# State-space mixer: the swap split from the state step and tied behind a GELU, four weight loads tied behind the returning quarters, the plan redrawn

## The chip, the cores and the metric

The kernel runs on one core of one Trainium2 chip. The metric is the device time of one execution in microseconds (us); several runs are taken and their median is compared. Beside the runs there is one profiled execution, from which every row below comes. TensorE is PE in the rows (PEld is its weight load), VectorE is DVE, ScalarE is ACT, GpSimd is POOL, and SyncE, which issues all the DMAs here, is SP.

## The reference

A two-layer decoder trunk on 512 tokens of width 1024, in float32: layer 0 mixes by convolution and attention, layer 1 by a state-space layer, and after each comes a gated MLP with a short convolution. The part around the change is the state-space mixer:

```python
u = (rms_norm(x) @ w_in).reshape(b, s, 32, 16)          # 512 wide, 32 groups of 16 channels
bu = einsum(u, B)                                       # each group feeds 64 complex states
x  = associative_scan(combine, (lam, bu))               # x[t] = lam * x[t-1] + bu[t], complex
y  = Re(C x) + D * u
y  = gelu(y)
z  = y @ w_glu + b_glu                                  # 512 -> 2048
return z[..., :1024] * sigmoid(z[..., 1024:])
```

## The kernel before

**Operands.** Every large weight comes in chunks of 128x1024 float32 (512 KB). `load_w` issues the DMA on SP into one of two `raw` buffers, `split_w` casts the chunk to a high part `whi` on ACT (three buffers) and takes the rest `wlo` on POOL in four pieces. Three matmuls (high by high, high by low, low by high) then stand for one float32 product. `chunk` hands out the chunks in a fixed order and keeps two loads ahead (`LOOK = 2`): after the last chunks of the first MLP come the four chunks of `w1` (the mixer's input projection), the eight of `wg` (the GLU), and then the second MLP. For a few chunks the cast is tied behind the newest ACT copy (`newest[0]`) at the point where the chunk is asked for.

**Who sets the order.** A scheduler orders the instructions of each engine by its own timeline. In the mixer all matmuls (`mm`) are held in program order, and `behind(a, b)` forces `a` after `b` on one engine without a wait between engines. Each engine, and SP's queue of DMAs, then works strictly in its order: an instruction that waits holds all behind it.

**The mixer in quarters.** The 512 channels are four quarters of eight groups. Time is cut into 64 chunks of 8 steps. For quarter q:

- dense: 24 matmuls of the input projection give `pss[q]` (quarters 0 and 1 run first, together, 48 matmuls; then quarter 2, then quarter 3);
- `s5_move`: ACT copies it to `u`, a DMA writes it to DRAM (`du`), and a second DMA (`moved[q]`) reads it back transposed into `rs[q]` (`r` in the rows); DVE scales it by the row norms (`s5_scale`);
- `E` (`s5_state`): 64 small matmuls on PE give `e1` and `e2`; DVE makes `za`, `zb`, their sum and the scan `z`; `swap` exchanges the two halves of the partitions with two ACT copies into `zs`; DVE makes `za`, `zs` (`turned`) and the state `xs`;
- `T` (`s5_direct`): 16 matmuls of `r` with table `tabT` into `y`; `O` (`s5_out`): 16 matmuls of `xs` with `tabO` added to `y`;
- `Y` (`s5_turn`): GELU on ACT (`ya`), 32 small matmuls that turn it (`yt`), then ACT and DVE split it into the operand of the GLU;
- `t` (`load_tables`): two DMAs of 512 KB each fetch the tables of quarter q, tied behind `moved[q]`.

**The plan.** A string gives the order on PE. `D24` means up to 24 more matmuls of the stream "dense projection of quarters 2 and 3, then GLU parts"; `A1`, `A2`, `A3` allow the GLU parts of quarter 0, 1, 2. The GLU parts are 12 matmuls of quarter 0, 12 of quarter 1, 6 and 6 more of these, and 18 of quarter 2. A `D` that meets a part which isn't allowed yet ends there. So in the plan before the dense runs are 24, 12, 6, 6, then 12, 12, 6, 6 (the second `D12` after `T3` stops at 6) and none after `O3`.

```python
PLAN = "D24 t1 E0 D12 t2 E1 T0 D6 O0 T1 D6 Y0 E2 t3 A1 D12 O1 Y1 T2 E3 A2 D12 O2 D6 Y2 T3 D12 O3 D12 Y3 A3"
```

After the plan the remaining GLU matmuls run, chunk by chunk, with the sigmoid and the product on ACT and DVE.

Of the kernel before, what the change touches and what calls it, by code (L numbers as in the profile page):

```python
# [38 lines left out]
E0 = 2  # L39
# [4 lines left out]

PLAN = "D24 t1 E0 D12 t2 E1 T0 D6 O0 T1 D6 Y0 E2 t3 A1 D12 O1 Y1 T2 E3 A2 D12 O2 D6 Y2 T3 D12 O3 D12 Y3 A3"
RA, RB2, GN = (26, 22, 6)
LAST = ("b", "sc", "pt", "b", "sc", "pt", "sc", "pt")
WT, WP, UT, UP = (8, 3, (2, 2, 1), (2, 1))  # L50
# [3 lines left out]
S0, S1 = (42, 16)  # L54
# [18 lines left out]
def trunk(ctx, tc, A, out):  # L73
    nc = tc.nc
    v, s, g, pe = nc.vector, nc.scalar, nc.gpsimd, nc.tensor
# [12 lines left out]
    def bank(name, tag=None):  # L88
        if tag is None:
            tag = CYCLE[turn[0] % len(CYCLE)]  # L90
            turn[0] += 1
        return pp.tile([128, T], F32, tag=tag, bufs=TAGS[tag], name=name)
# [4 lines left out]
    def tmp(name="t", shape=(128, T), dt=F32):  # L97
        return tp.tile(list(shape), dt, tag="t", bufs=6, name=name)
# [4 lines left out]
    def behind(ins, first):  # L103
        tc.add_manual_dep(ins.ins, first.ins.name, mybir.DependencyInfo(
            mybir.DependencyClass.NoSync, mybir.DependencyReason.DATA), reason="order on one engine")
# [3 lines left out]
    def mm(*a, **kw):  # L109
        r = pe.matmul(*a, **kw)  # L110
        return held(r) if fixed[0] else r

    def load_w(src, n):
        raw = wp.tile([128, 1024], F32, tag="raw", bufs=WB, name="raw")
        nc.sync.dma_start(out=raw[:, :n * 128], in_=src)
        return raw

    def split_w(raw, n, eng=None, keep=None, after=None):
        if keep:
            hi, lo = (keep.tile([128, n, 128], F32R, tag=t, bufs=KD - 1, name=t) for t in ("khi", "klo"))  # L120
        else:
            hi = wp.tile([128, 8, 128], F32R, tag="whi", bufs=3, name="whi")
            lo = wp.tile([128, 8, 128], F32R, tag="wlo", bufs=3, name="wlo")
        r = raw[:, :n * 128].rearrange("p (k m) -> p k m", m=128)
        cast = s.copy(hi[:, :n], r)  # L125
        if after:
            behind(cast, after)
        for a in range(0, n, 2):
            (eng or g).tensor_tensor(lo[:, a:a + 2], r[:, a:a + 2], hi[:, a:a + 2].bitcast(F32), ALU.subtract)  # L129
        return hi, lo  # L130

    order = [(A["w0"][m], 8) for m in range(12)]
    order += [(A["wukv"], 8), (A["wuq"][0], 8), (A["wuq"][1], 8)]
    order += [(A[n][c], 8) for n, c in (("wo_a", 0), ("wo_a", 1), ("wo_a", 2), ("wo_c", 0), ("wo_a", 3),
# [10 lines left out]
    first_w1 = len(order)  # L145
# [8 lines left out]
    def chunk(src, n=8):  # L154
        i = taken[0]
        assert order[i][1] == n and order[i][0].tensor is src.tensor and order[i][0].offset == src.offset
        if i == first_w1 + 2:
            queue[i + 1] = split_w(queue[i + 1], 8, after=newest[0])
        while len(queue) <= min(i + LOOK, len(order) - 1):
            j = len(queue)  # L160
            raw = load_w(*order[j])
            if j == first_w1 + 3:
                queue.append(raw)
                continue
            queue.append(split_w(raw, order[j][1], keep=kept[0] if stay <= j < stay + KD - 1 else None,
                                 after=newest[0] if first_w1 + 2 <= j <= first_w1 + 6 else None))
        taken[0] += 1
        res, queue[i] = queue[i], None
        return res
# [24 lines left out]
    for step in START:  # L194
        if step[0] == "x":
            k = int(step[1])
# [82 lines left out]
    def xhi():  # L279
        return xp.tile([128, T], F32R, tag="xh", bufs=8, name="xh")  # L280

    def xlo():
        return xp.tile([128, T], F32R, tag="xl", bufs=8, name="xl")
# [75 lines left out]
    for step in START:  # L359
        if step[0] == "x":  # L360
            k = int(step[1])
# [15 lines left out]
    with tc.tile_pool(name="l0", bufs=1) as lp:  # L377
        def slot(name, dt=F32):
            return lp.tile([128, T], dt, tag="m", bufs=16, name=name)
# [3 lines left out]
        def w_in(m):  # L383
            fill(WT, WP)
            if m in early:
                return early[m]
            return proj(bank("win", ("sc", "b")[m % 2]), chunk(A["w0"][m]), n0.hl)
# [107 lines left out]
        for i in range(2):  # L495
            ps = w_in(M_Q + i)
            t = slot(f"cq{i}")
# [20 lines left out]
        for t in (cq[0], cq[1], ckv):  # L518
            q = tmp("sq")
# [126 lines left out]
        for i in range(4):  # L646
            v.scalar_tensor_tensor(y[i], mb, -1.0 / CW, y[i], ALU.mult, ALU.add)
            q = tmp("sq")
# [303 lines left out]
    def ztmp(name):  # L952
        return fp.tile([128, T], F32, tag="z", bufs=ZB, name=name)
# [50 lines left out]
                elif extra:  # L1004
                    extra.pop(0)()

    tTs, tOs, moved = [], [], {}

    def load_tables(q):
        gq = slice(8 * q, 8 * q + 8)  # L1010
        for lst, n in ((tTs, "T"), (tOs, "O1")):
            t = fp.tile([128, 8, 128], F32, tag="ghl", bufs=GB, name="tab" + n)
            d = nc.sync.dma_start(out=t, in_=park[n][:, gq])
            if q:
                behind(d, moved[max(q, 1)])
            lst.append(t)
# [6 lines left out]
    tE, tC, tS, tD = tab["E"], tab["C"], tab["S"], tab["D"]  # L1023

    def as_g(t):
        return t.rearrange("p (g c) -> p g c", c=NC)

    lo, hi = slice(0, 64), slice(64, 128)
    pss, rs, xs, yb, ys = {}, {}, {}, {}, []
    late, done_r = [], []  # L1030

    def s5_move(q):
# [11 lines left out]
    def s5_scale(q):  # L1044
        v.tensor_tensor(rs[q], rs[q], rowr.unsqueeze(1).to_broadcast([128, 8, NC]), ALU.mult)

    def swap(dst, src):
        s.copy(dst[lo], src[hi])
        newest[0] = s.copy(dst[hi], src[lo])

    def s5_state(q):
        gq = slice(8 * q, 8 * q + 8)
        cf, sf = (t[:, gq].rearrange("p g c -> p (g c)") for t in (tC, tS))
        e1, e2 = bank("e1", "b"), bank("e2", "b")
        for e, other in ((e1, (lo, hi)), (e2, (hi, lo))):
            for i in range(8):
                for a, to in zip((lo, hi), other):
                    mm(e[to, i * NC:(i + 1) * NC], tE[:, 8 * q + i, a], rs[q][:, i], start=True, stop=True)
        za, zb, z, zs = ztmp("za"), ztmp("zb"), ztmp("z"), ztmp("zs")
        v.tensor_tensor(za, e1, cf, ALU.mult)  # L1060
        v.tensor_tensor(zb, e2, sf, ALU.mult)
        v.tensor_tensor(za, za, zb, ALU.add)
        v.tensor_tensor_scan(z, tD[:, gq].rearrange("p g c -> p (g c)"), za, 0.0, ALU.mult, ALU.add)
        swap(zs, z)
        x_ = ztmp("xs")
        xs[q] = as_g(x_)
        g.memset(xs[q][:, :, 0:1], 0.0)
        v.tensor_tensor(za, z, cf, ALU.mult)
        turned(zs, sf)
        v.tensor_tensor(xs[q][:, :, 1:], as_g(za)[:, :, :NC - 1], as_g(zs)[:, :, :NC - 1], ALU.subtract)  # L1070

    def turned(t, sf):
        v.tensor_tensor(t, t, sf, ALU.mult)
# [7 lines left out]
    def s5_direct(q):  # L1081
        yb[q] = bank("y", "pt")
        table(yb[q], tTs[q], rs[q], True, False)

    def s5_out(q):
        table(yb[q], tOs[q], xs[q], False, True)

    def s5_turn(q):
        ya = tmp("ya")
        gelu = s.activation(ya.rearrange("p (j g c) -> p g j c", j=CL, c=GC),  # L1090
                     yb[q].rearrange("p (g j c) -> p g j c", j=CL, c=GC), AF.Gelu_apprx_tanh)
        if q == 3:
            behind(s.activation(spot[:, 129:130], spot[:, :1], AF.Sigmoid), gelu)
        yt = bank("yt", "pt")
        for j in range(CL):
            for h, a in enumerate((lo, hi)):
                mm(yt[a, j:T:CL], ya[:, 64 * j:64 * j + 64], ident[:, a], start=(j == 0), stop=(j == CL - 1))
        h, l = xhi(), xlo()
        s.copy(h, yt)
        v.tensor_tensor(l, yt, h.bitcast(F32), ALU.subtract)  # L1100
        ys.append((h, l))
# [40 lines left out]
    def dense(n):  # L1142
        while n > 0 and next(more, False) is not False:
            n -= 1
# [16 lines left out]
    behind(s.activation(spot[:, 128:129], spot[:, :1], AF.Gelu_apprx_tanh), newest[0])  # L1161
    for step in PLAN.split():
        k, n = step[0], int(step[1:])
        if k == "t":
            load_tables(n)
        elif k == "E":
            s5_state(n)
        elif k == "T":
            s5_direct(n)
        elif k == "O":  # L1170
            s5_out(n)
        elif k == "Y":
            s5_turn(n)
        elif k == "D":
            dense(n)
        elif k == "A":
            allow[0] = n
# [3 lines left out]
    for m in range(KD):  # L1181
# [8 lines left out]
        t = tmp("gz")  # L1190
# [167 lines left out]
```

## Time and profile before

| | us |
|---|---|
| median of 3 runs | 1056.7 |
| the runs | 1058.8, 1055.66, 1056.7 |
| profiled execution, its own time | 1060.18 |
| span of the profiled execution | 1058.5 |

The rows of a timeline give start, length, engine, line, operation, output from inputs, shape, count, and in brackets the idle time before it with what ended it. Lengths of matmuls are modelled and overlap: the price of a block of matmuls is read from start to start of the next block. All matmuls of the mixer carry the line of the helper `mm`, L110, so they are told apart by tile: `w` dense, `e` state, `y` from `tabT` or `tabO`, `yt` turn, `gl` GLU.

### The profile page before, as it was taken

What the parts mean: (1) busy time and instruction counts of PE and PEld (TensorE: products, weight loads), DVE (VectorE), ACT (ScalarE), POOL (GpSimd) and SP (SyncE); (2) the same over time, 40 slices, a digit from 0 to 9 for tenths busy, and PEclk for the clock granted to TensorE, in tenths of its full rate; (3) what the DMA queues carried; (4) which work ended last, traced back from release to release, by engine and by line L of the source; (5) the groups of instructions that cost most, each with busy time, mean ns of one, the idle gap of its engine ahead of it and who ended that gap; (6) DMA issues with size and microseconds to landing.
All of it is one profiled execution on the core that took longest, in us unless ns stands there. A gap on an engine that the chain in (4) does not pass through costs nothing.

```text
span 1058.5 us, 14208 instructions
## 1 busy us (share of the span) xinstructions
PE 1022.6 (97%) x5094; PEld 828.9 (78%) x5094; DVE 637.9 (60%) x1081; ACT 450.8 (43%) x675; POOL 679.4 (64%) x822
## 2 busy tenths in 40 slices
PE   7998999999999999999999979999999999999996
PEld 4876567888888888777888767888888888888895
DVE  7679973676499688889444663777421444214435
ACT  5566975535421434323444423635421444224431
POOL 4898965677666877778755622767655666556750
PEclk9999999999999999999999989999999999999998
DMA  6232202423223333333324550323323233233222
GB/s 199 97 113 80 61 21 57 125 100 118 89 93 95 100 124 104 98 118 99 119 82 138 176 165 21 120 82 115 101 80 104 96 100 100 90 109 100 88 72 80
DMA packets 50005, 106.63 MB, mean 101 GB/s; under 512 B 16400, under 2 KB 24336, under 8 KB 49936
## 3 DMA queue, kind: packets, MB, share of 16 engines
q1 hardware_dynamic: 49936, 105.74, 31.4%
q8 instruction: 40, 0.66, 0.3%
q14 instruction: 29, 0.24, 0.1%
HBM read 97.33 MB, written 7.34 MB: 99 GB/s over the span
## 4 chain that ended last, share of the span: by engine, by line
PE 76%; DVE 12%; ACT 4%; DMA 3%; issue 2%; POOL 2%; SPq 1%; DVEq 0%; POOLq 0%; ACTq 0%
PE ua L110 19%; PE dn L110 19%; PE ug L110 19%; PE wo L110 4%; PE gl L110 4%; PE win L110 3%; DVE acc L432 2%; PE pv L612 1%; PE sc L582 1%; ACT whi L125 1%; PE w L110 1%; POOL wlo L129 1%; DVE ug L968 1%; DVE ua L968 1%; PE pt L596 1%
## 5 line engine op out<-in xcount | busy, mean ns | idle before, releaser
L129 POOL TENSOR_TENSOR wlo<-raw,whi 128x256 fp32r<-128x256 f32 x639 | 492.1, 803 | 250.8 <-ACT whi L125 222.9
L125 ACT CAST whi<-raw 128x1024 fp32r<-128x1024 f32 (+1 forms) x162 | 167.3, 1037 | 266.8 <-PE dn L110 98.0
L110 PE MATMUL dn<-ghl,whi 128*128 128x512 f32 (+1 forms) x632 | 193.7, 389 | 0.3 <-ACT ghl L985 0.3
L110 PEld LDWEIGHTS dn<-ghl,whi 128*128 128x128 f32 x632 | 118.1, 189 | 25.2 <-ACT ghl L985 0.7
L110 PE MATMUL ua<-xh,whi 128*128 128x512 f32 x352 | 137.4, 390 | 0.0
L110 PE MATMUL ug<-xh,whi 128*128 128x512 f32 x352 | 137.4, 390 | 0.0
L110 PE MATMUL ug<-xl,whi 128*128 128x512 f32 x352 | 137.1, 389 | 0.0
L110 PE MATMUL ua<-xh,wlo 128*128 128x512 f32 x352 | 137.0, 389 | 0.0
L110 PE MATMUL ug<-xh,wlo 128*128 128x512 f32 x352 | 136.9, 389 | 0.0
L110 PE MATMUL ua<-xl,whi 128*128 128x512 f32 x352 | 136.9, 389 | 0.0
L110 PE MATMUL dn<-ghl,wlo 128*128 128x512 f32 (+1 forms) x316 | 122.2, 387 | 0.0
L968 DVE SCALAR_TENSOR_TENSOR ug<-h,vec,ug 128x511 f32<-128x511 f32 x88 | 66.3, 754 | 49.9 <-ACT ug L966 48.3
L968 DVE SCALAR_TENSOR_TENSOR ua<-h,vec,ua 128x511 f32<-128x511 f32 x88 | 66.3, 753 | 44.3 <-ACT ua L966 42.9
L986 POOL TENSOR_TENSOR ghl<-g,ghl 128x512 fp32r<-128x512 f32 x44 | 57.3, 1303 | 39.1 <-ACT ghl L985 36.2
L110 PEld LDWEIGHTS ug<-xh,whi 128*128 128x128 f32 x352 | 66.1, 188 | 14.5 <-issue 0.6
L110 PEld LDWEIGHTS ua<-xh,wlo 128*128 128x128 f32 x352 | 66.1, 188 | 13.8
L110 PEld LDWEIGHTS ug<-xh,wlo 128*128 128x128 f32 x352 | 66.1, 188 | 13.8
L110 PEld LDWEIGHTS ua<-xh,whi 128*128 128x128 f32 x352 | 66.0, 188 | 13.8 <-issue 0.2
L110 PEld LDWEIGHTS ua<-xl,whi 128*128 128x128 f32 x352 | 66.1, 188 | 13.5
L110 PEld LDWEIGHTS ug<-xl,whi 128*128 128x128 f32 x352 | 66.1, 188 | 13.4
L998 DVE TENSOR_TENSOR x<-x,dn 128x512 f32<-128x512 f32 x40 | 26.7, 681 | 80.6 <-PE dn L110 80.5
L110 PEld LDWEIGHTS dn<-ghl,wlo 128*128 128x128 f32 x316 | 59.8, 189 | 12.1
(334 smaller groups left out, 1743.2 us busy)
## 6 DMA issues: line engine op xcount, KB each, us to landing
raw<-up SPq DMA_DIRECT2D x88, 512.0 KB, 3.5
raw<-down SPq DMA_DIRECT2D x32, 512.0 KB, 3.5
raw<-w SPq DMA_DIRECT2D x14, 512.0 KB, 3.6
raw<-down SPq DMA_DIRECT2D x16, 384.0 KB, 3.0
raw<-wg SPq DMA_DIRECT2D x8, 512.0 KB, 3.6
raw<-wo_a SPq DMA_DIRECT2D x4, 512.0 KB, 3.5
raw<-wo_c SPq DMA_DIRECT2D x4, 512.0 KB, 3.6
park_O<-wn SPq DMA_DIRECT2D x8, 256.0 KB, 2.4
```

The source lines that it names most:

```text
L110: r = pe.matmul(*a, **kw)
L125: cast = s.copy(hi[:, :n], r)
L129: (eng or g).tensor_tensor(lo[:, a:a + 2], r[:, a:a + 2], hi[:, a:a + 2].bitcast(F32), ALU.subtract)
L432: held(v.scalar_tensor_tensor(acc[:, sh:], u[:, :T - sh], col("cw", i * CK + CK - 1 - sh), acc[:, sh:], ALU.mult, ALU.add))
L582: pe.matmul(ps[:, :L], q[:, sl], k[:, :L], start=True, stop=False)
L596: pe.transpose(pt[:, kt * 128:(kt + 1) * 128], p[:, kt * 128:(kt + 1) * 128], ident)
L612: pe.matmul(ps[a, kt * 128:], vv[:, kt, i * 128 + 64 * e:i * 128 + 64 * e + 64], pts[e][:, 4 * kt:3 * kt + 4].rearrange("p k c -> p (k c)" ...
L968: v.scalar_tensor_tensor(ps[:, sh:], t[:, :T - sh], col(fw, 3 * j + 2 - sh), ps[:, sh:], ALU.mult, ALU.add)
L986: g.tensor_tensor(lo, gt, h.bitcast(F32), ALU.subtract)
L998: done = v.tensor_tensor(x[m], x[m], ps, ALU.add)
```

## The change

Four edits. `s5_state` ends after the scan, and what followed (the swap, the products, `xs`) becomes `s5_carry`, a step `S` of its own in the plan. The first copy of a quarter's swap is tied behind the newest GELU, if there is one. The loads of the first four `wg` chunks are tied on SP's queue behind the read-back DMAs `moved[0]` to `moved[3]`. The plan is redrawn: its dense runs are now 27, 4, 7, 6, 4, then 12, 12, 12, and none after `O3` (the `D18` there meets a part that isn't allowed yet). No instruction is added or taken away.

```diff
-PLAN = "D24 t1 E0 D12 t2 E1 T0 D6 O0 T1 D6 Y0 E2 t3 A1 D12 O1 Y1 T2 E3 A2 D12 O2 D6 Y2 T3 D12 O3 D12 Y3 A3"
+PLAN = "D27 t1 E0 S0 D4 E1 T0 D7 O0 t2 D6 Y0 S1 D4 t3 E2 T1 O1 A1 D12 Y1 S2 E3 T2 O2 A2 D12 Y2 S3 T3 D12 O3 D18 Y3 A3"
...
-    def load_w(src, n):
+    def load_w(src, n, after=None):
         raw = wp.tile([128, 1024], F32, tag="raw", bufs=WB, name="raw")
-        nc.sync.dma_start(out=raw[:, :n * 128], in_=src)
+        d = nc.sync.dma_start(out=raw[:, :n * 128], in_=src)
+        if after:
+            behind(d, after)
         return raw
...
+    moved = {}
...
-            raw = load_w(*order[j])
+            raw = load_w(*order[j], after=moved.get(j - first_w1 - 4))
...
-    tTs, tOs, moved = [], [], {}
+    tTs, tOs = [], []
...
-    pss, rs, xs, yb, ys = {}, {}, {}, {}, []
+    pss, rs, xs, yb, ys, zq, gelus = {}, {}, {}, {}, [], {}, []
...
-    def swap(dst, src):
-        s.copy(dst[lo], src[hi])
+    def swap(dst, src, first):
+        part = s.copy(dst[lo], src[hi])
+        if first:
+            behind(part, first)
         newest[0] = s.copy(dst[hi], src[lo])
...
         v.tensor_tensor_scan(z, tD[:, gq].rearrange("p g c -> p (g c)"), za, 0.0, ALU.mult, ALU.add)
-        swap(zs, z)
+        zq[q] = za, z, zs
+
+    def s5_carry(q):
+        gq = slice(8 * q, 8 * q + 8)
+        cf, sf = (t[:, gq].rearrange("p g c -> p (g c)") for t in (tC, tS))
+        za, z, zs = zq.pop(q)
+        swap(zs, z, gelus[-1] if gelus else None)
         x_ = ztmp("xs")
         xs[q] = as_g(x_)
         g.memset(xs[q][:, :, 0:1], 0.0)
...
+        gelus.append(gelu)
...
+        elif k == "S":
+            s5_carry(n)
```

## Rows read from the trace of the kernel before

**Rows 1.** The page: busy time of each engine with its share of the span and its instructions, and the granted TensorE clock in 40 slices of the span (tenths of full speed).

```profile
PE 1022.6 (97%) x5094; PEld 828.9 (78%) x5094; DVE 637.9 (60%) x1081; ACT 450.8 (43%) x675; POOL 679.4 (64%) x822
PEclk9999999999999999999999989999999999999998
```

**Rows 2.** The view by stretches, all engines. Columns: the stretch, its length, busy us (and instructions) of PE, PEld, DVE, ACT and POOL, the granted TensorE clock, DMA share, GB/s.

```profile
614.00:618.10 4.10, 1.94 (x14) 1.17 (x10) 3.41 (x5) 2.32 (x4) 0.11 (x1) 1.00 0.68 249
625.10:629.00 3.90, 0.08 (x4) 0.04 (x2) 2.98 (x4) 2.77 (x4) 0.45 (x1) 0.80 0.23 96
629.00:635.30 6.30, 6.30 (x113) 6.23 (x113) 1.38 (x2) 0.59 (x1) 2.55 (x5) 0.58 0.27 86
654.60:690.00 35.40, 35.23 (x154) 28.41 (x153) 24.40 (x29) 20.84 (x31) 28.20 (x31) 1.00 0.32 105
```

**Rows 3.** The timeline of TensorE through the mixer, merged: start, length, what, count, idle before and what ended it.

```profile
602.96 2.09 PE L110 MATMUL e<-r,tabE 128*64 128x64 f32 x64 [0.95 <-DVE r L1045]
604.97 0.50 PE L110 MATMUL w<-xh,whi 128*128 128x512 f32 x1
...
607.92 2.08 PE L110 MATMUL e<-r,tabE 128*64 128x64 f32 x64
609.83 1.05 PE L110 MATMUL y<-tabT,r 128*64 128x128 f32 x16
610.81 0.50 PE L110 MATMUL w<-xh,whi 128*128 128x512 f32 x1
...
612.39 1.09 PE L110 MATMUL y<-tabO,xs 128*64 128x128 f32 x16
613.32 1.04 PE L110 MATMUL y<-tabT,r 128*64 128x128 f32 x16
...
618.14 1.15 PE L110 MATMUL yt<-ident,ya 128*64 128x64 f32 x32 [2.20 <-ACT ya L1090]
619.12 2.04 PE L110 MATMUL e<-r,tabE 128*64 128x64 f32 x64
621.09 0.50 PE L110 MATMUL gl<-xh,whi 128*128 128x512 f32 x1
...
628.97 1.98 PE L110 MATMUL yt<-ident,ya 128*64 128x64 f32 x32 [3.82 <-ACT ya L1090]
630.73 1.92 PE L110 MATMUL y<-tabT,r 128*64 128x128 f32 x16
632.43 2.87 PE L110 MATMUL e<-r,tabE 128*64 128x64 f32 x64
635.24 0.50 PE L110 MATMUL gl<-xh,whi 128*128 128x512 f32 x1
...
644.33 1.09 PE L110 MATMUL y<-tabO,xs 128*64 128x128 f32 x16
646.12 1.15 PE L110 MATMUL yt<-ident,ya 128*64 128x64 f32 x32 [0.70 <-ACT ya L1090]
```

**Rows 4.** The timeline of ScalarE in the same stretch, the rows around the swaps and the GELUs.

```profile
607.80 0.62 ACT L1048 COPY zs<-z 64x512 f32<-64x512 f32 x1 [5.18 <-DVE z L1063]
...
609.07 1.05 ACT L125 CAST whi<-raw 128x1024 fp32r<-128x1024 f32 x1
...
617.00 0.58 ACT L1034 COPY u<-w 128x512 f32<-128x512 f32 x1
617.49 0.60 ACT L1090 ACTIVATE ya<-y 128x512 f32<-128x512 f32 x1
...
626.10 0.62 ACT L1048 COPY zs<-z 64x512 f32<-64x512 f32 x1 [6.18 <-DVE z L1063]
...
627.37 1.04 ACT L125 CAST whi<-raw 128x1024 fp32r<-128x1024 f32 x1
628.32 0.59 ACT L1090 ACTIVATE ya<-y 128x512 f32<-128x512 f32 x1
```

**Rows 5.** The timeline of VectorE: the state of quarter 0 (`xs`) and the scaling of quarter 3 (`r`).

```profile
610.29 1.18 DVE L1070 TENSOR_TENSOR xs<-za,zs 128x504 f32<-128x504 f32 x1
...
622.73 0.69 DVE L1045 TENSOR_TENSOR r<-r,spot 128x512 f32<-128x512 f32 x1 [1.49 <-DMA r<-du]
```

**Rows 6.** The timeline of SP's queue, start and length of an issue (not of the transfer): the loads of `wg` chunks 0, 1, 2 and 4, and write and read-back of quarters 2 and 3.

```profile
592.93 0.33 SPq L115 DMA_DIRECT2D raw<-wg  x1
...
602.29 0.33 SPq L115 DMA_DIRECT2D raw<-wg  x1
602.73 0.78 SPq L1036 DMA_DIRECT2D du<-u  x1
605.95 0.33 SPq L115 DMA_DIRECT2D raw<-wg  x1
609.88 0.32 SPq L1038 DMA_DIRECT2D r<-du  x1
...
617.62 0.37 SPq L1036 DMA_DIRECT2D du<-u  x1
...
619.96 0.32 SPq L1038 DMA_DIRECT2D r<-du  x1
...
631.52 0.33 SPq L115 DMA_DIRECT2D raw<-wg  x1
```

**Rows 7.** The DMA view of 602.2 to 602.5 us alone, which holds the load of `wg` chunk 1: KB, and us from issue to landing.

```profile
raw<-wg SPq DMA_DIRECT2D x1, 512.0 KB, 6.6
```

## The prediction

> **What bounds the kernel now.** I read the page first. TensorE is busy 97% of the span, and the granted clock is full but for one slice of 40 inside it, the 24th (609 to 635 us), and the last [rows 1]. So the kernel is bound by TensorE nearly everywhere, and time can only come from places where it idles or runs slowly. The view by stretches finds them: of 614.0 to 618.1 TensorE is busy 1.94 us of 4.10, of 625.1 to 629.0 almost none, and from 629.0 to 635.3 it is busy throughout at a mean clock of 0.58, mostly the lower of its two levels, 1.2 GHz [rows 2]. That is the state-space mixer. The timeline of TensorE names the releasers: 0.95 us before E0 (scaled quarter 0), 2.20 us before the first turn and 3.82 us before the second (both a GELU), 0.70 us before the fourth [rows 3]. Last comes the timeline of ScalarE: when quarter 1 has its output, about 625.1, the GELU doesn't run; the engine stands idle 6.18 us until the swap of quarter 2 can start at 626.10, then casts a weight chunk (1.04 us), and only then runs the GELU, at 628.32 [rows 4]. The same at the first turn: a swap and the copy of quarter 3 stand ahead of the GELU at 617.49. These two waits, with the slow stretch behind the second, are what the change aims at.
>
> **The slow stretch.** Turn, T and E take 1.76, 1.70 and 2.81 us from start to start there, and 0.98, 0.98 and 1.97 at full clock [rows 3]: 6.27 against 3.93, so 2.34 us are lost. It followed an idle time of 3.82 us; the idle time of 2.20 us left the clock at 1.00 [rows 2].
>
> **The change, part by part.** No instruction comes or goes; the edits move order alone, so each is costed by who waits. From start to start, E costs 1.91 to 2.01 us, T 0.98, O 0.93, a turn 0.98, 12 dense matmuls 2.95 and 6 of them 1.58 (0.23 each plus 0.21 of switching) [rows 3]. With these I walk the new plan.
>
> E0 waits as before for scaled quarter 0 and starts at 602.96, but three more matmuls run ahead of it: 3 x 0.23 = 0.68 of the 0.95 us is covered. E0 ends 604.97, D4 606.1, E1 608.0, T0 609.0, D7 610.8. O0 now comes early and needs `xs` of quarter 0, which was done at 611.47 (610.29 plus 1.18) [rows 5]; I put it at 611.9, for a reason given with the loads, so O0 stands 1.1 us. This is the new wait. Its floor is nothing (the 5.18 us before that quarter's swap [rows 4] are mostly DVE's chain, in which the step of quarter 1 may stand elsewhere), its ceiling 4.4 (first rival).
>
> O0 ends 612.85, the GELU of 0.60 us [rows 4] is done by 613.5 under D6, which ends 614.4: the wait of 2.20 us is gone. Turn 615.4, D4 616.5, E2 (1.97) 618.5, T1 619.5, O1 620.4. The second GELU is done by 621.0 under D12, which ends 623.4: the wait of 3.82 is gone, and with no idle time above 2.20 I expect no slow stretch, so the 2.34 too. Turn 624.4, E3 626.4, T2 627.3, O2 628.3, D12 631.2, turn 632.2, T3 633.2, D12 636.1. From O3 to the fourth turn it was 1.79 us (644.33 to 646.12, with the 0.70 of waiting) [rows 3] and stays so: 637.9 against 646.12, 8.2 us earlier with the same matmuls done. The ledger of waits says 0.68 + 2.20 + 3.82 + 2.34 - 1.1 = 7.9. I take 8.0.
>
> The tie of the swaps costs nothing as long as gelu(q-1) is early: they end 613.5, 621.0 and 628.9. Quarter 2's swap started 5.0 us after the end of its E, 1.49 of that a wait for quarter 3 [rows 3 to 5], so the swaps could start without the tie at about 612 to 613, 622 to 623.5 and 630 to 631.5. The tie holds only the first, by about a microsecond. From swap to the end of `xs` quarter 0 took 3.67 us (607.80 to 611.47) [rows 4, 5], so `xs` is ready by 617.2, 627.2 and 635.2 at the latest, for O at 619.5, 627.3 and 636.1. What waits behind a tied swap on ScalarE are casts and the copies of quarters; O(q), with the dense runs, T and E ahead of it, is the cover. Without it, each late microsecond is one on the path.
>
> The loads: the load of GLU chunk 0 went out at 592.93 into an idle queue; now it stands behind the read-back of quarter 0, so at about 599.5, ahead of the first tables and of quarter 2's write. Chunk 2 (605.95) leaves the stretch ahead of quarter 2's read-back [rows 6]. A price is shown by quarter 2's write: 7.15 us (602.73 to 609.88) behind other transfers, 2.34 for quarter 3's (617.62 to 619.96) [rows 6]. Chunk 1 landed at 608.9 (602.29 + 6.6) [rows 6, 7], and 256 KB of quarter 2 took the 0.98 us after it, so 512 KB more in front are worth 1 to 2 us: I take 1.5, with nothing as the other bound, since chunk 2 leaves. Read-back 1 then lands up to 1.5 us later; its scaling stands ahead of the first product of E0 on VectorE and pushes that chain by some 0.4 (the 611.9 above). Quarter 2's read-back goes out at 611.4, lands 2.8 later like quarter 3's (619.96 to 622.73) [rows 5, 6], is scaled (0.69) by 614.9, and E2 starts at 616.5: covered, by 1.6. The Trainium skill says in "DMA: Bandwidth & Descriptors", section on queues, rings and completion order, that each DMA engine takes descriptors in ring order; by that the full 1.5 holds, while with fair sharing chunk 2's leaving would pay for chunk 0's coming and O0 would stand 0.7, a gain of 8.4.
>
> Quarter 3 is the tight one. Its last dense matmul falls at about 616.4, its copy at 617.0 as before [rows 4], so its scaled read-back is there at 623.4 as before [rows 5], and E3 now wants it at 624.4 instead of 632.43. Cover 1.0 us; beyond that every microsecond counts.
>
> One more bound for O0: quarter 0's `xs` took 1.18 beside a split on POOL where an operation of this kind takes 0.69 [rows 5], and chunk 0's split moves onto that quarter's chain. If three operations of the chain paid 0.5 each, O0 would stand 2.6 and the gain be 6.5. The Trainium skill, "SBUF — State Buffer", section on its two separate sides, says that a VectorE operation with two SBUF inputs waits for the whole of a GpSimd operation on the port they share; the row of 1.18 agrees, and by that rule the 6.5 is as likely as the 8.0.
>
> After the mixer TensorE is busy 35.23 of 35.40 us and the next weights follow its progress [rows 2], so the shift passes to the end whole. The sum against the profiled execution: 1060.18 - 8.0 = 1052.2 of its own time. That run stands 3.5 above the median, so in the median 1056.7 - 8.0 = 1048.7.
>
> **The rivals.** First, chunk 1's cast takes the place of the wait removed. Before, it was tied behind quarter 0's swap (609.07 after 607.80) [rows 4]; in the new plan that chunk is asked for within D27, before S0, so it is tied only behind quarter 2's copy and may be put ahead of the swap. With chunk 1 landing 1.5 later, at 610.4, and the cast at 1.05, the swap starts 611.5 instead of 607.8 and O0 at about 615.2 or less: 3.3 us lost over my sum, and as O0 would then stand some 4.4 us, more than 3.82, the clock falls and 2.34 more go. Gain 2.4, 1054.3. For it: the guard is gone. Against: the scheduler knows that loads take time, and z of quarter 0 is ready at 607.8, before the chunk landed even in the old order.
>
> Second, quarters 2 or 3 come back late: 1 to 3 us beyond their cover of 1.6 and 1.0. Gain 5 to 7 with one stall; where it passes the 3.82 of the old one, 2.34 more go and 2 to 4 are left: 1050 to 1055.
>
> Third, on the other side: chunk 4's load, which nobody ties, gets ahead of quarter 3's read-back on SP. It waits until chunk 2's split frees the `raw` buffer; before, it went out at 631.52 at that instant [rows 6]. Queued ahead, it holds the read-back until the split ends, and E3 starts 0.1 + 2.8 + 0.7 = 3.6 later. Against 624.4 with the 2.34 of the clock, nothing is left of the 8.0 once the split ends after 626.5, and it is slower by over 0.3% (about what a measurement of this kernel can tell, 3.2 us) after 629.7. At the old 631.5 E3 starts at 635.1: 10.7 + 2.34 - 8.0 = 5.0 slower, 1061.7. Against: chunk 2's cast is now asked for after quarter 3's copy, near 617, and its split should end near 624.
>
> Fourth, the change does nothing, since the scheduler puts other work ahead of the GELUs again (chunk 2's cast stood there before [rows 4]) and the waits return in other places: 1055 to 1058.
>
> **How the numbers follow.** My forecast has 0.57 (its own range 1047 to 1051: O0 standing 0 to 2.6, and the microsecond of the runs), the first rival 0.15, the second 0.10, the third 0.08, the fourth 0.10. Faster by over 0.3%: 0.57, most of the first two, 0.78. Within 0.3%: 0.13, from the fourth, with bits of the first and third. Slower: 0.09, mostly the third. The range holds the forecast and the first two rivals: 1046.5 to 1055.5.
>
> **What would show it.** Right: the turns of quarters 0 and 1 start with no idle time before them, the fourth near 638; clock 1.00 throughout 600 to 640; ScalarE runs GELU, then swap; O0 has a wait of about 1 us for `xs`. Wrong: a cast ahead of quarter 0's swap and O0 after 614 (first); E2 or E3 waiting for the scaled `r` (second), with a `wg` load just ahead of the last read-back (third); a GELU again behind a swap or a cast (fourth).

## The result

The changed kernel takes 1051.19 us in the median of 7 runs (1048.78 to 1052.97), the kernel before 1056.27 beside it (1055.32 to 1060.09). The ratio over all these runs is 0.9948, with a 95% interval of 0.9933 to 0.9963: 5.5 us less, between 3.9 and 7.1 (the two medians alone stand 5.1 apart). Forecast were 8.0 less and 1048.7.

The page of the changed kernel, busy time and granted clock, against [rows 1]:

```profile
PE 1019.8 (97%) x5094; PEld 827.6 (79%) x5094; DVE 634.8 (60%) x1081; ACT 451.3 (43%) x675; POOL 682.2 (65%) x822
PEclk9999999999999999999999999999999999999998
```

The dent in the clock is gone from the slices, each of which is a mean over 26 us. The timeline of TensorE in the mixer (start, length, idle before), against [rows 3]:

```profile
601.57 2.08 PE L110 MATMUL e<-r,tabE 128*64 128x64 f32 x64
...
604.78 2.09 PE L110 MATMUL e<-r,tabE 128*64 128x64 f32 x64
...
611.58 1.98 PE L110 MATMUL y<-tabO,xs 128*64 128x128 f32 x16 [2.02 <-issue]
...
615.73 1.15 PE L110 MATMUL yt<-ident,ya 128*64 128x64 f32 x32
...
624.67 1.15 PE L110 MATMUL yt<-ident,ya 128*64 128x64 f32 x32
625.65 2.04 PE L110 MATMUL e<-r,tabE 128*64 128x64 f32 x64
...
639.00 1.15 PE L110 MATMUL yt<-ident,ya 128*64 128x64 f32 x32 [0.69 <-ACT ya L1101]
```

The first two turns (615.73 and 624.67) start with no idle time ahead; they had waited 2.20 and 3.82 us. The new wait is the one named: O0 stands 2.02 us. But a slow stretch follows it, as the view by stretches shows (the last three columns are clock, DMA share, GB/s):

```profile
609.40:611.58 2.18, 0.16 (x1) 0.03 (x1) 2.18 (x4) 0.00 (x0) 2.18 (x3) 0.99 0.46 165
611.58:615.73 4.15, 4.15 (x22) 3.12 (x23) 3.53 (x5) 1.83 (x3) 0.53 (x2) 0.60 0.94 344
...
647.00:683.00 36.00, 35.84 (x157) 29.03 (x156) 25.11 (x30) 21.96 (x32) 29.09 (x32) 1.00 0.32 103
```

What stands ahead of O0 is seen on three engines. ScalarE (first rows), VectorE and SP's queue, against [rows 4 to 6]:

```profile
607.02 1.05 ACT L127 CAST whi<-raw 128x1024 fp32r<-128x1024 f32 x1 [4.25 <-DMA raw<-wg]
608.09 0.62 ACT L1051 COPY zs<-z 64x512 f32<-64x512 f32 x1
...
613.59 0.60 ACT L1101 ACTIVATE ya<-y 128x512 f32<-128x512 f32 x1 [4.25 <-PE y L110]
614.38 0.62 ACT L1051 COPY zs<-z 64x512 f32<-64x512 f32 x1 [0.19 <-DVE z L1068]
...
621.82 0.60 ACT L1101 ACTIVATE ya<-y 128x512 f32<-128x512 f32 x1 [2.25 <-PE y L110]
623.38 0.62 ACT L1051 COPY zs<-z 64x512 f32<-64x512 f32 x1 [0.97 <-DVE z L1068]
```
```profile
603.31 0.82 DVE L1048 TENSOR_TENSOR r<-r,spot 128x512 f32<-128x512 f32 x1 [2.23 <-DMA r<-du]
...
606.09 1.64 DVE L1068 TENSOR_TENSOR_SCAN z<-tabD,za 128x512 f32<-128x512 f32 x1
...
610.81 0.67 DVE L1081 TENSOR_TENSOR xs<-za,zs 128x504 f32<-128x504 f32 x1
```
```profile
597.98 0.38 SPq L115 DMA_DIRECT2D raw<-wg  x1
598.46 0.38 SPq L1041 DMA_DIRECT2D r<-du  x1
...
621.59 0.32 SPq L1041 DMA_DIRECT2D r<-du  x1
...
622.96 1.23 SPq L115 DMA_DIRECT2D raw<-wg  x2
```

Chunk 0's load went between the read-backs of quarters 0 and 1. The second of these, issued at 598.46, let VectorE go on only at 603.31, 4.8 us later, and all products of quarter 0 stood behind its scaling. Then the cast of chunk 1 stood ahead of quarter 0's swap for 0.36 us (`z` was done at 607.73). `xs` was done at 611.48. Further on, the rows show the GELU ahead of the next quarter's swap twice, as wanted.

**A measure for the experiments.** From start to start, the stretch from the row-norm matmul (`rowr`, ahead of the plan) to the fourth turn is the mixer alone. What lies behind it agrees to 0.4 us in the profiles of these two kernels (412.38 us before, 412.30 after). What lies ahead doesn't: the orders of instructions up to there are the same but for chunk 0's load, yet `rowr` starts between 591.32 and 596.13 in the profiles below. So a single profiled execution moves by some us for reasons outside the mixer.

### The profile page after: what moved, and what is told of

It reads as the page before. It is cut to its first block, busy times and chain, and to the rows that moved or that the text cites. A ratio compares the mean times of both kernels' runs of the same rounds, so it can differ in the third digit from the quotient of the medians.

```text
span 1051.3 us, 14211 instructions
## 1 busy us (share of the span) xinstructions
PE 1019.8 (97%) x5094; PEld 827.6 (79%) x5094; DVE 634.8 (60%) x1081; ACT 451.3 (43%) x675; POOL 682.2 (65%) x822
## 4 chain that ended last, share of the span: by engine, by line
PE 79%; DVE 12%; ACT 4%; issue 2%; DMA 1%; POOL 1%; SPq 1%; DVEq 0%; ACTq 0%; POOLq 0%
PE ua L110 20%; PE dn L110 19%; PE ug L110 19%; PE wo L110 4%; PE gl L110 4%; PE win L110 3%; PE w L110 2%; DVE acc L435 2%; PE pv L615 1%; PE sc L585 1%; ACT whi L127 1%; DVE ug L971 1%; DVE ua L971 1%; PE y L110 1%; PE pt L599 1%
## 5 line engine op out<-in xcount | busy, mean ns | idle before, releaser
L971 DVE SCALAR_TENSOR_TENSOR ug<-h,vec,ug 128x511 f32<-128x511 f32 x88 | 66.4, 754 | 49.3 <-ACT ug L969 47.7
L971 DVE SCALAR_TENSOR_TENSOR ua<-h,vec,ua 128x511 f32<-128x511 f32 x88 | 66.3, 753 | 44.0 <-ACT ua L969 42.6
```

The costliest lines, as they stand in the source:

```text
L971: v.scalar_tensor_tensor(ps[:, sh:], t[:, :T - sh], col(fw, 3 * j + 2 - sh), ps[:, sh:], ALU.mult, ALU.add)
```

## The experiments

**One: the two kernels again.** A second profile of the kernel before, one of the kernel after, and the kernel after without the tie of the swaps.

> The kernel before once more, for a second profile. If the slow stretch of 2.34 us behind the second turn belongs to the order of its instructions, it is there again behind the wait of 3.8 us. If it is a matter of the single execution, it may be missing or stand elsewhere; then the profiled execution of before, 3.5 us above the median, carried a loss that the median need not have, and the gain against the median had to come out smaller than the sum.

> The changed kernel once more, beside the mended one on one chip. 1050 to 1052; O0 waits 1.8 to 2.1 us, and whether the slow clock follows is open: in one profile of this order of instructions it did, in another it didn't.

> The changed kernel without the tie of the swaps (load ties and new plan kept). Theory A: in the new plan the step S of a quarter comes behind the turn of the one before, so the swap stands behind the GELU with or without the tie: the order of every engine is the same, the time is that of the changed kernel, 1050.5 to 1052, O0 again waits 2.0 us, and the slow clock behind it may or may not come again. Rival: the tie holds the order, and without it the GELU of quarter 1 is late by 3 us and 2.3 us of slow clock follow: 1055 to 1057.

```diff
-        swap(zs, z, gelus[-1] if gelus else None)
+        swap(zs, z, None)
```

Without the tie the order of all engines comes out the same as with it, instruction for instruction: in the new plan a step S stands behind the turn of the quarter before, and the scheduler puts the swap behind the GELU without being told. It is a third execution of the changed order: 1050.14 in the median, ratio 0.9943 (0.9922 to 0.9965). The changed kernel again: 1051.35, 0.9948 (0.9933 to 0.9962). The timeline and the stretches behind the wait, first the kernel before again:

```profile
626.92 1.15 PE L110 MATMUL yt<-ident,ya 128*64 128x64 f32 x32 [3.83 <-ACT ya L1090]
```
```profile
626.92:630.80 3.88, 3.88 (x113) 3.81 (x113) 1.38 (x2) 0.59 (x1) 2.59 (x5) 1.00 0.12 21
```

The same wait of 3.83 us, and no slow stretch: the turn, T and E behind it take 3.88 us at clock 1.00, where they took 6.27 [rows 3]. Then the changed kernel again, and the one without the tie:

```profile
610.13 1.09 PE L110 MATMUL y<-tabO,xs 128*64 128x128 f32 x16 [1.57 <-issue]
```
```profile
610.13:612.75 2.62, 2.62 (x23) 1.90 (x23) 2.62 (x3) 0.60 (x1) 0.54 (x2) 1.00 0.94 327
```
```profile
607.93 1.09 PE L110 MATMUL y<-tabO,xs 128*64 128x128 f32 x16 [1.84 <-issue]
```
```profile
607.93:610.55 2.62, 2.62 (x23) 1.91 (x23) 2.62 (x3) 0.60 (x1) 0.53 (x2) 1.00 0.92 321
```

Again the wait without the slow clock: 2.62 us against 4.15, so the first profile of the changed kernel lost 1.53 there.

| execution | `rowr` | fourth turn | mixer | slow clock cost | at full clock |
|---|---|---|---|---|---|
| before | 596.13 | 646.12 | 49.99 | 2.34 | 47.65 |
| before again | 593.91 | 641.62 | 47.71 | 0 | 47.71 |
| after | 595.08 | 639.00 | 43.92 | 1.53 | 42.39 |
| after again | 593.77 | 636.04 | 42.27 | 0 | 42.27 |
| after, no swap tie (same order) | 591.32 | 633.84 | 42.52 | 0 | 42.52 |

So the change is worth 5.2 to 5.4 us at full clock (47.7 to 42.3 or 42.5), and 5.5 in the runs. The waits of the old order aren't fixed either: E0 and the first turn waited 0.95 and 2.20 in its first profile, 0.34 and 3.00 in its second.

**Two: which part carries it.** Both ties with the old plan, and the old dense runs with only the swaps moved (loads not tied, both halves of a swap tied).

> Both ties kept, the plan put back to the old one, with each step S right behind its E. Theory A: the swap of quarter 2 is tied only behind the GELU of quarter 0, so the GELU of quarter 1 still waits for it; the second turn waits 3 to 4 us and the slow stretch follows: 1054.5 to 1057.5. Rival: the ties carry the gain, the plan little: 1050.5 to 1052.

```diff
-PLAN = "D27 t1 E0 S0 D4 E1 T0 D7 O0 t2 D6 Y0 S1 D4 t3 E2 T1 O1 A1 D12 Y1 S2 E3 T2 O2 A2 D12 Y2 S3 T3 D12 O3 D18 Y3 A3"
+PLAN = "D24 t1 E0 S0 D12 t2 E1 S1 T0 D6 O0 T1 D6 Y0 E2 S2 t3 A1 D12 O1 Y1 T2 E3 S3 A2 D12 O2 D6 Y2 T3 D12 O3 D12 Y3 A3"
```

> The old plan with its old dense runs, loads not tied; only the steps S of quarters 2 and 3 moved behind the turns of quarters 1 and 2, with both halves of the swap tied behind the GELU. Theory A: the second turn's wait falls from 3.8 to under 1 us and the slow stretch goes, the first turn still waits 2.2 us: gain 5 to 6 us, 1050.5 to 1051.5. Rival C: the redrawn dense runs carry the gain, and with the old ones another wait follows at O1 or O2: 1054 to 1057.

```diff
-PLAN = "D27 t1 E0 S0 D4 E1 T0 D7 O0 t2 D6 Y0 S1 D4 t3 E2 T1 O1 A1 D12 Y1 S2 E3 T2 O2 A2 D12 Y2 S3 T3 D12 O3 D18 Y3 A3"
+PLAN = "D24 t1 E0 S0 D12 t2 E1 S1 T0 D6 O0 T1 D6 Y0 E2 t3 A1 D12 O1 Y1 S2 T2 E3 A2 D12 O2 D6 Y2 S3 T3 D12 O3 D12 Y3 A3"
...
-            raw = load_w(*order[j], after=moved.get(j - first_w1 - 4))
+            raw = load_w(*order[j], after=None)
...
         newest[0] = s.copy(dst[hi], src[lo])
+        if first:
+            behind(newest[0], first)
```

The ties with the old plan: 1057.98, ratio 1.0006 (0.9993 to 1.0020), nothing gained; the mixer takes 48.09 us with a slow stretch, worth some 1.5, that stands behind the first turn this time; the second turn waits 2.42, less than the 3 to 4 of theory A. The swaps alone: 1053.12, 0.9967 (0.9954 to 0.9980), the mixer 44.38 with no slow stretch. First and second turn, of the one and of the other:

```profile
615.19 1.97 PE L110 MATMUL yt<-ident,ya 128*64 128x64 f32 x32 [2.69 <-ACT ya L1101]
...
626.07 1.15 PE L110 MATMUL yt<-ident,ya 128*64 128x64 f32 x32 [2.42 <-ACT ya L1101]
```
```profile
616.58 1.15 PE L110 MATMUL yt<-ident,ya 128*64 128x64 f32 x32 [2.78 <-ACT ya L1103]
...
624.29 1.15 PE L110 MATMUL yt<-ident,ya 128*64 128x64 f32 x32 [0.69 <-ACT ya L1103]
```

As theory A had it, the swap ahead of the GELU, with the cast that was tied behind it, was the second wait: moved away, the wait falls from 3.83 to 0.69, and the mixer by 3.3 us against the second profile of before. The gain of 5 to 6 that I expected had the slow stretch in it again; 3.5 were measured. The other 2.0 us of the change (44.38 to 42.4) come with the redrawn dense runs, less what the load ties, which this run doesn't have, take back: the dense runs cover the first turn, and open the wait at O0. A run further down that differs from this one in the plan alone (guard, no load tie) takes 41.40.

**Three: what is late at O0.** First the load tie taken out of the changed kernel.

> The changed kernel with the four weight loads no longer tied to the read-backs (swap tie and new plan kept). Theory A: the gain comes from the second GELU standing ahead of the swap, and the load tie costs, because the load of GLU chunk 0 goes between the read-backs of quarters 0 and 1, the scaling of quarter 1 then holds VectorE, and O0 waits 2.0 us with a slow clock behind it. Without the tie quarter 1 is scaled right behind quarter 0, O0 waits under 1.2 us, the clock stays full, and the time is 2 to 3 us below the changed kernel, 1048.0 to 1049.5. Rival B: the load tie is what brings the quarters back in time; without it E2 or E3 waits 1 to 3 us and the time is 1052 to 1055.

```diff
-            raw = load_w(*order[j], after=moved.get(j - first_w1 - 4))
+            raw = load_w(*order[j], after=None)
```

1051.79, ratio 0.9950 (0.9931 to 0.9969): no difference from the changed kernel. Theory A missed here, and rival B too. The mixer takes 44.10 us, 1.53 of them slow clock (O0 to the first turn is 4.15 us again), and O0 waits 2.29, for another reason (TensorE, ScalarE, POOL):

```profile
610.35 1.44 PE L110 MATMUL y<-tabO,xs 128*64 128x128 f32 x16 [2.29 <-POOL xs L1078]
...
605.36 1.05 ACT L127 CAST whi<-raw 128x1024 fp32r<-128x1024 f32 x1 [5.21 <-DMA raw<-wg]
...
610.18 0.15 POOL L1078 MEMSET xs<- 128x8 f32 x2
```

Quarter 1 is scaled right behind quarter 0 now, but chunk 1's cast stands ahead of quarter 0's swap and delays it by 1.09 us, and on POOL the small memset of quarter 0's `xs` stands behind that chunk's split. Each late part hides the other, so I took both away: three dense matmuls moved behind S0 let chunk 1 be asked for there, and its cast is tied behind the swap as before the change; then the same without the load tie.

> The changed kernel with three dense matmuls moved from ahead of E0 to ahead of E1 (24 and 7 instead of 27 and 4), so that GLU chunk 1 is asked for behind S0 and its cast is tied behind quarter 0's swap again; both halves of a swap tied. Theory D: the 2 us at O0 are made of quarter 1's late scaling (1.3 us, from chunk 0's load between the read-backs) and the cast ahead of the swap (0.4 here, 1.1 in the run without load tie). E0 waits up to 0.9 us again, O0 under 1.2 us, no slow clock; from the row-norm matmul to the fourth turn 41.8 to 42.6 us (before 50.0, changed 43.9 with and 42.5 without a slow clock). Rival E: the products of quarter 1, which now come early and stand between those of quarter 0 on VectorE, are what is late; then O0 keeps 1.5 us or more.

```diff
-PLAN = "D27 t1 E0 S0 D4 E1 T0 D7 O0 t2 D6 Y0 S1 D4 t3 E2 T1 O1 A1 D12 Y1 S2 E3 T2 O2 A2 D12 Y2 S3 T3 D12 O3 D18 Y3 A3"
+PLAN = "D24 t1 E0 S0 D7 E1 T0 D7 O0 t2 D6 Y0 S1 D4 t3 E2 T1 O1 A1 D12 Y1 S2 E3 T2 O2 A2 D12 Y2 S3 T3 D12 O3 D18 Y3 A3"
...
         newest[0] = s.copy(dst[hi], src[lo])
+        if first:
+            behind(newest[0], first)
```

> As the last, with the loads not tied either. Theory D: quarter 1 is scaled right behind quarter 0 and no cast stands ahead of the swap, so O0 waits 0.5 us or less; 41.2 to 42.0 us from the row-norm matmul to the fourth turn. Rival E: O0 still waits over 1.2 us.

```diff
-            raw = load_w(*order[j], after=moved.get(j - first_w1 - 4))
+            raw = load_w(*order[j], after=None)
```

With the load tie 1050.80, 0.9937 (0.9917 to 0.9958), the mixer 44.09 us; without it 1048.92, 0.9920 (0.9891 to 0.9949), the mixer 41.40. Rows of VectorE and TensorE, with the tie and without:

```profile
606.12 1.05 DVE L1048 TENSOR_TENSOR r<-r,spot 128x512 f32<-128x512 f32 x1 [4.12 <-DMA r<-du]
...
607.82 2.08 PE L110 MATMUL e<-r,tabE 128*64 128x64 f32 x64 [1.78 <-DVE za L1067]
...
614.15 1.09 PE L110 MATMUL y<-tabO,xs 128*64 128x128 f32 x16 [1.55 <-issue]
```
```profile
598.74 1.83 DVE L1048 TENSOR_TENSOR r<-r,spot 128x512 f32<-128x512 f32 x2 [4.79 <-DMA r<-du]
...
608.62 1.09 PE L110 MATMUL y<-tabO,xs 128*64 128x128 f32 x16 [0.45 <-issue]
```

With the tie VectorE stands 4.12 us for the read-back of quarter 1, and both E1 and O0 wait; without it O0 waits 0.45. So with both late parts gone the wait is nearly gone, as theory D had it. Rival E, the early products of quarter 1, falls as the main cause: they stand in the same place in the second run, where one of them holds `xs` back by 0.60 us. The run with the tie missed its forecast: O0 kept 1.55, 1.78 came at E1, and the mixer took 44.09 instead of 41.8 to 42.6. The reason is the read-back, issued at 599.34, seen in the DMA view (KB, and us from issue to landing) of the changed kernel, the run with both ties and the old plan, and this run:

```profile
r<-du SPq DMA_DIRECT2D x1, 256.0 KB, 4.8
```
```profile
r<-du SPq DMA_DIRECT2D x1, 256.0 KB, 3.9
```
```profile
r<-du SPq DMA_DIRECT2D x1, 256.0 KB, 6.8
```

In the six other profiles with chunk 0's load just ahead of it, quarter 1's read-back landed after 3.9 to 4.8 us, in the six without after 2.6 to 3.6. The 6.8 stands alone. Both tables of quarter 1 followed right behind it here (599.78 and 600.25), but so they did in the run with the old plan, which has the same order on SP up to there and took 3.9: the tables aren't the reason, and what was stays open. So the 2.7 us between the two mixers are not the price of the load tie, and most of them may be this execution's; the medians differ by 1.9, and their intervals overlap. How much of the wait at O0 is the load's and how much the cast's these runs don't separate.

**Four: fill the wait instead.**

> The changed kernel with seven more dense matmuls ahead of O0 (14 there, 3 behind it, none behind the first turn). They cover 1.6 us of O0's wait. But here the second half of quarter 1's swap, which the change doesn't tie, stands ahead of the first GELU on ScalarE, so that GELU waits for the scan of quarter 1: O0 under 0.7 us, first turn 1.0 to 2.5 us of waiting, 42 to 43.5 us from the row-norm matmul to the fourth turn. Rival: the half left untied is harmless and the stretch is 41.0 to 41.8 us.

```diff
-PLAN = "D27 t1 E0 S0 D4 E1 T0 D7 O0 t2 D6 Y0 S1 D4 t3 E2 T1 O1 A1 D12 Y1 S2 E3 T2 O2 A2 D12 Y2 S3 T3 D12 O3 D18 Y3 A3"
+PLAN = "D27 t1 E0 S0 D4 E1 T0 D14 O0 t2 D3 Y0 S1 t3 E2 T1 O1 A1 D12 Y1 S2 E3 T2 O2 A2 D12 Y2 S3 T3 D12 O3 D18 Y3 A3"
```

> As the last, with both halves of a swap tied behind the GELU. O0 waits under 0.7 us, the first turn under 0.5 us, the clock stays full, 41.0 to 41.8 us from the row-norm matmul to the fourth turn; in the median 1048.5 to 1050. If the two kernels take the same, the half left untied cost nothing.

```diff
         newest[0] = s.copy(dst[hi], src[lo])
+        if first:
+            behind(newest[0], first)
```

Half tied 1051.47, 0.9956 (0.9937 to 0.9974), mixer 43.09; both halves tied 1049.87, 0.9934 (0.9910 to 0.9958), mixer 42.39. O0 waits in neither; the first turn does (ScalarE and TensorE of the first, TensorE of the second):

```profile
610.81 0.62 ACT L1054 COPY zs<-z 64x512 f32<-64x512 f32 x1 [5.24 <-DVE z L1068]
...
612.59 1.15 PE L110 MATMUL yt<-ident,ya 128*64 128x64 f32 x32 [2.59 <-ACT ya L1101]
```
```profile
612.39 1.15 PE L110 MATMUL yt<-ident,ya 128*64 128x64 f32 x32 [1.17 <-ACT ya L1103]
...
624.55 1.09 PE L110 MATMUL y<-tabO,xs 128*64 128x128 f32 x16 [0.61 <-issue]
```

In the first the second copy of quarter 1's swap (L1054), which the change leaves untied, stands ahead of the GELU and waits for that quarter's scan: the tie holds half a swap. With both halves tied the wait falls by 1.4 us in the profile, but the mixer only by 0.7, since O2 now stands 0.61 (the second row); the intervals of the times overlap. The 1.17 left, which I hadn't expected, is the copy of quarter 3, which now comes ahead of the GELU since its last dense matmul stands ahead of O0. So the mixer takes 42.39, not the 41.0 to 41.8 forecast.

**Five: the plan mended where the runs found waits.**

> The new plan mended where the runs found waits: 24 dense matmuls ahead of E0 (chunk 1's cast tied behind quarter 0's swap), 9 instead of 7 ahead of O0, the GLU parts of quarter 2 allowed ahead of the fourth turn (six of them there), loads not tied, both halves of a swap tied. Of the 41.4 us that the run with the guard and no load tie took from the row-norm matmul to the fourth turn, the 0.45 us at O0 and the 0.70 us at the fourth turn go; the six GLU matmuls that now stand ahead of the turn (1.6 us) are missing behind it. So from the row-norm matmul to the fourth turn about 41.9, and from there to the end 1.6 less than 412.3; 1047 to 1048.5 in the median. If a wait comes back elsewhere: 1048.5 to 1050.

```diff
-PLAN = "D27 t1 E0 S0 D4 E1 T0 D7 O0 t2 D6 Y0 S1 D4 t3 E2 T1 O1 A1 D12 Y1 S2 E3 T2 O2 A2 D12 Y2 S3 T3 D12 O3 D18 Y3 A3"
+PLAN = "D24 t1 E0 S0 D7 E1 T0 D9 O0 t2 D4 Y0 S1 D4 t3 E2 T1 O1 A1 D12 Y1 S2 E3 T2 O2 A2 D12 Y2 S3 T3 D12 O3 A3 D6 Y3"
...
-            raw = load_w(*order[j], after=moved.get(j - first_w1 - 4))
+            raw = load_w(*order[j], after=None)
...
         newest[0] = s.copy(dst[hi], src[lo])
+        if first:
+            behind(newest[0], first)
```

1049.31 in the median, ratio 0.9921 (0.9904 to 0.9937) to the kernel before: 8.3 us less than before, and about 2 below the changed kernel's second set on the same chip (1051.35). The forecast of 1047 to 1048.5 missed; its other branch, a wait that comes back elsewhere at 1048.5 to 1050, is what came. O0 and the fourth turn start without idle time. The mixer takes 42.72 us with six GLU matmuls more in it; what lies behind it is 1.4 shorter, so 41.3 on the old measure, hardly below the 41.40 of the run with guard and no load tie. The gain came back as a wait elsewhere (TensorE, VectorE):

```profile
623.80 2.09 PE L110 MATMUL e<-r,tabE 128*64 128x64 f32 x64 [0.93 <-DVE r L1048]
```
```profile
622.00 1.04 DVE L1081 TENSOR_TENSOR za<-z,tabC 128x512 f32<-128x512 f32 x1
622.97 0.68 DVE L1048 TENSOR_TENSOR r<-r,spot 128x512 f32<-128x512 f32 x1
```

E3 now waits for the scaled quarter 3. Its read-back, issued at 619.67, took 2.7 us and was there at 622.4; the scaling began only at 622.97, when VectorE had done a product of quarter 2 that took 1.04 instead of 0.69 beside a split on POOL. So up to 0.6 of the 0.93 is VectorE's queue, and the rest the way of the quarter itself.

## Why the prediction was right, and where it wasn't

**The GELU behind the swap: right.** Both turns lost their waits, the swaps stand behind the GELUs, and moving the swaps alone takes the second wait down to 0.69. That the tie itself costs nothing was right for a reason I hadn't seen: in this plan it changes no order. The microsecond by which it was to hold the first tied swap didn't come: in all three profiles of this order that swap waited for its scan (0.19, 1.07 and 1.08 us), not for the GELU.

**The slow stretch: the step that failed.** I put the 2.34 us of slow clock into the sum as if the wait of 3.82 made it each time, and said that without idle time above 2.20 us there would be none. The same order of the kernel before ran at full clock behind a wait of 3.83, and the changed kernel once lost 1.53 behind 2.02 and twice nothing behind 1.84 and 1.57. So the profiled execution of before carried a loss that its second profile doesn't have, and I took the sum off the median, from which that execution stood 3.5 us away; a part of that distance was this very term. Without it the forecast is 5.7 instead of 8.0. (The clock of 1.00 that I read for the wait of 2.20 is that of the wait itself; behind it the turn took 0.98, so it was full there too.) How often the unprofiled runs have a slow stretch isn't known. What the clock's fall depends on beyond the wait ahead of it the runs don't tell. The Trainium skill says in "TensorE: Matmul & The Clock Gate", Part 1, that the clock gate's watch runs on freely and doesn't start with the kernel, so that one kernel shows different numbers of slow matmuls from run to run. These profiles agree in that one order of instructions differs from run to run, though behind a wait in its middle; why it does they don't show.

**O0: right in place, short in size.** I had 1.1 us of waiting; 1.57 to 2.02 were measured, inside the 0 to 2.6 of the text. The price of 512 KB ahead of a read-back, taken as 1.5 us, held: 3.9 to 4.8 us to landing with the load ahead, 2.6 to 3.6 without (the 6.8 of one run apart). That the Trainium skill's "DMA: Bandwidth & Descriptors" has descriptors taken in ring order (section on queues, rings and completion order) goes with this: in the changed kernel the read-back was issued 0.48 us behind the load and landed after it. What was too small is what the chain on VectorE made of it. Set to the times of the profile before by `rowr`, D7 ended at 610.6 to 610.9 in the three profiles of this order, as forecast (610.8), but `xs` was done at 612.4 to 612.6, not 611.9. The first product of quarter 0 was 0.2 to 1.0 later than in that profile (0.4 forecast), and from there to `xs` it took 0.1 to 0.7 longer, a term that I had at nothing: the cast ahead of the swap (0.36, 0.14 and 0.78 us) and operations beside a split on POOL (0.6 to 1.3 us longer together, the scan 1.64 in all three, where the profile before paid 0.5 in `xs`).

**The first rival** came in part: chunk 1's cast did go ahead of quarter 0's swap, for 0.36 us of delay in the changed kernel and 1.09 without the load tie, not for the 3.7 of the text, since the chunk landed at 607.0, or 608.1 in the times of the profile before (whose `rowr` is 1.05 later), and not at 610.4.

**The rest.** E0's wait (0.27 forecast) was 0, 0.28 and 0.28 in the three profiles of this order. E2 and E3 didn't wait in the changed kernel, with quarter 3 scaled at 624.34 to 625.03 for an E3 at 625.65: the cover was 0.6 us, where 1.0 was forecast, and the mended plan used it up (0.93 us of waiting at E3, more of it VectorE's than the read-back's). The third rival didn't come: chunk 4's load went out behind quarter 3's read-back (622.96 after 621.59). The wait of 0.7 at the fourth turn stayed, and the shift passed to the end whole. With the 2.34 gone, 0.5 to 0.9 more at O0 and, in one profile, 0.3 less at E0, 8.0 becomes 4.9 to 5.2, against the 5.2 to 5.4 between the mixers at full clock. The measured 1051.2 lies just above the forecast's own 1047 to 1051; it is inside the whole range only by the room left for two rivals that didn't come as told, which is luck.

## What to carry to other kernels

Before a slow stretch in one profile goes into a sum, ask for a second profile of the same kernel: the wait is the order's, the slow clock behind it may be the execution's. Take a sum that starts from one execution off that execution only, and say which of its terms the median shares. A load that is moved behind a transfer to let it pass will be in front of the next one; and when two causes end at the same wait, taking away one shows nothing until the other is gone as well.

## What the hardware showed that I hadn't expected

Two executions of one order of instructions, each with an idle time of 3.8 us at the same place, ran on at a mean clock of 0.58 in one and 1.00 in the other; an idle time of 2.02 was followed by a mean clock of 0.60, one of 3.00 (the first turn of before, second profile) by 1.00. Over all profiles here a slow stretch followed waits of 2.02, 2.29, 2.69 and 3.82 us, and none followed waits of 2.42, 2.59, 2.78, 3.00 and 3.83: the length of the wait alone doesn't decide it. And with nothing changed ahead of the mixer, its start moved by 4.8 us between profiles.
